# First loads, product with ones, order of a merge and last scaling of a two-layer hybrid trunk on one Trainium2 core

## Chip, core and metric

The kernel runs on one NeuronCore of one Trainium2 chip, with five engines beside the 16 DMA engines: TensorE (PE in the profile; its weight loads are PEld), VectorE (DVE), ScalarE (ACT), GpSimd (POOL) and SyncE (SP, which here only issues DMAs). The metric is the device time of one launch in microseconds; lower is better. All arithmetic is fp32, or fp32 split into two parts (below).

## What is computed

Two layers over x (1 x 512 x 1024), each a token mixer with three branches and a gated MLP, and a final RMSNorm:

```python
for l in range(2):
    h = rmsnorm(x, norm1_g[l])
    p = h @ w_in[l]                      # 1024 -> 1792 + 1536 + 1024 + 3072
    y_rw  = rwkv7_branch(p_rw, ...)      # scan over 512 steps, 8 heads of 64
    y_ret = retention_branch(p_ret, ...) # chunks of 128, 4 heads
    y_sg  = sgu_branch(p_sg, ...)        # gating with a causal 128 x 128 matrix per group, + bias
    branches = stack([y_rw, y_ret, y_sg])
    proj  = einsum('bsgc,gcd->bsgd', branches, w_branch[l])     # 512 -> 1024 each
    gates = sigmoid(gate_logits)
    x = x + sum(gates * proj, axis=2) @ w_out[l]
    x = x + conv_ffn(rmsnorm(x, norm2_g[l]), ...)               # 1024 -> 5632 -> 1024
return rmsnorm(x, final_g)
```

In `sgu_branch` the vector v is normalised over its 512 channels with `sg_ln_g` and `sg_ln_b` and then mixed by the masked matrix w; the constant `sg_ln_b` comes through the mixing as the row sums of w times `sg_ln_b`.

## The kernel before

**Layout.** Activations lie transposed, features on the 128 partitions and the 512 positions along the row; x is eight blocks of 128 x 512. A product of fp32 values is made of three fp32r matmuls: each operand is split into a high part (a cast on ACT, L127, L136 or L202) and a low part (the difference, on DVE, L128, L137 or L203), and `mm3` (L140) adds high x low, high x high and low x high in PSUM. Some small products stay fp32 (the transposes, the ones product at L848, retention's chunks).

**Weights** stream in units of 128 x 512 floats (256 KB). `load` (L112) issues a unit's DMA on SP's queue into one of three raw buffers `wr`; `part` (L120) splits it. `unit` (L89) keeps loads and splits a few units ahead of PE by a plan that a first pass over the program records. The tile framework's scheduler then sets the order of the instructions on each engine; what is wrapped in `keep_in_program_order` (`self.kept`, `po`) or in `high_priority` keeps its written place. Semaphores are placed by the framework wherever two engines touch a tile; tiles of a pool are handed out again in turn, so a new tile waits for the last user of the buffer's old one. PSUM has four accumulators `acc` and four small tiles `sm`.

**Start (`run`, L258).** DVE fills `rst` with ones, and PE runs six fp32 products on it as a warm-up (L269). `load_pc(0)` (L304) brings the layer's 250 columns of per-channel factors (norm gains, mixing factors, decay factors and so on; `pc`, 125 KB) on ACT's queue; behind it x1 and x3 go on ACT's queue, the other x blocks and the first weights on SP's. Then a step list written out by hand sets the order on ACT and DVE: `z` is a block of `norm_z` (L199: x times gain, split), `w` a weight split, `s` a square and its sum (`norm_sq`, L206). The sums go into `norm_stats` (L216), a product with ones on PE, in the middle of the first projection (`firstF`, L233). At the top of `rwkv` (L384) five small DVE products make derived factors from `pc` (`omu`, `haw`, `hka`, `oka`, `nkk`; L390 to L398). L505 later writes zeros into some columns of `rst`, which the scan uses as its reset mask.

**Mixer (L308).** While the recurrence's small products run, PE is filled with projections. Then come the spatial gating's values (`sgu_v`), its bias (`sgu_bias`, L843), the recurrence's output, and the merge, whose order is a step list at L332:

```python
for step in "S S 0 0 R U S 0 R 0 U S 0 0 R 0 0 R 2 2 Y 2 1 2 1 2 1 2 1 2 1 2 1 1 1".split():
```

`S` is a group of spatial gating, `R` a chunk of retention (`ret_chunk`, L754; small fp32 products, with normalisation through ACT, DVE and a power on GpSimd at L781), `U` two units of a projection, `Y` the transposition and split of retention's heads (`ret_out`, L802, transposes at L807). `0`, `2` and `1` are blocks of `merge` (L864) for the recurrence, the spatial gating and retention: the gate values come by a DMA on GpSimd's queue (L868), twelve matmuls go into an `acc`, DVE multiplies by the gate (L871), and `2` adds to the block's sum on GpSimd, `1` on DVE (L874). A block `1` needs `Y`.

`sgu_bias` multiplies the masked 128 x 4 x 128 gating matrix `ws` by a 128 x 128 tile of ones in one fp32 product; `ws` is masked at L325.

**End (`finish`, L945).** The last of the eight output blocks of the second MLP is computed in two halves of 256 positions, so that the first half's normalisation runs beside the second half's matmuls. For a half, `stats` sums the squares and takes the power -1/2 on GpSimd (L974), `out` spreads the result over the partitions by transposes into the PSUM tile `pb` (L980), and `scale` forms eight products x * gain * pb on DVE (L986), each sent out by a 128 KB DMA, alternately on ACT's and SP's queue (L987).

Of the kernel before, what the change touches and what calls it, by code (L numbers as in the profile page):

```python
# [17 lines left out]
S = 512  # L18
# [28 lines left out]
class Emit:  # L47
# [210 lines left out]
    def run(self):  # L258
        nc, tc, a, V = self.nc, self.tc, self.a, self.nc.vector
        self.con = self.cp.tile([128, NCC], F32, name="con")  # L260
        self.rst = self.cp.tile([128, 512], F32, name="rst")
        self.bonesR = self.cp.tile([128, 128], F32R, name="bonesR")
        self.ones = self.cp.tile([128, 128], F32, name="ones")
        V.memset(self.rst, 1.0)
        V.memset(self.ones, 1.0)
        nc.scalar.copy(self.small((128, 1), "ms"), self.rst[:, 0:1])
        wu = self.acc()
        for i in range(6):
            nc.tensor.matmul(wu[:, 0:256], self.rst[:, 0:128], self.rst[:, 256:512], start=True, stop=True)  # L269
        self.load_pc(0)  # L270
        st = self.norm_new()
        xs = [self.u(n="x") for _ in range(8)]
        self.keep = True
        with tc.high_priority():
            for j in range(8):
                tc.keep_in_program_order((nc.scalar if j in (1, 3) else nc.sync).dma_start(xs[j], a["xT"][:, j, :]))
                if self.plan and j in (0, 2, 3):
                    self.load(self.plan[self.nraw])
        for step in "z0 w z1 z2 w z3 w z4 z5 w z6 z7 w s0 s1 s2 w s3 s4 s5 s6 s7".split():
            if step == "w":  # L280
                if self.plan:
                    if self.nraw == self.npart:
                        self.load(self.plan[self.nraw])
                    self.part(self.plan[self.npart])
            elif step[0] == "z":
                self.norm_z(st, xs[int(step[1])], "n1")
            else:
                self.norm_sq(st, xs[int(step[1])])
        self.keep = False
        tc.keep_in_program_order(nc.scalar.dma_start(self.con, a["con"]))  # L290
        xd = [a["xT"][:, j, :] for j in range(8)]
        for l in range(L):
            mg = self.mixer(l, st)
            st = self.norm_new()
            x = self.wout(l, mg, xd, st)
            act = self.ffn_up(l, st)
            st = self.norm_new()
            x, xd = self.ffn_down(l, act, x, st)
            if l == L - 1:
                self.finish(l, act, x, st["acc"])  # L300
            self.rp.__exit__(None, None, None)
            self.fp = None
# [5 lines left out]
    def mixer(self, l, nst):  # L308
        self.pool = None
        with self.tc.tile_pool(name=f"rw{l}", bufs=1) as rp:  # L310
            self.rwp = rp
            self.filler = self.fillers(l)
            st = self.rwkv(l, nst)
        for _ in self.filler:
            pass
        self.rp = self.tc.tile_pool(name=f"ff{l}", bufs=NFP)
        self.fp = self.rp.__enter__()
        self.gup, self.bs, self.ws = self.f(n="gup"), self.f((128, 4, 128), n="bs"), self.f((128, 4, 128), n="ws")
        with self.tc.high_priority():
            self.nc.sync.dma_start(self.gup, self.a["gup"][l])  # L320
        self.nc.sync.dma_start(self.bs.rearrange("p g i -> p (g i)"), self.a["sgb"][l:l + 1, :].to_broadcast([128, 512]))
        self.nc.sync.dma_start(self.ws, self.a["sgw"][l])
        self.pool = "f"
        sg, out = self.sgu_v(l), self.rwkv_out(l, *st)
        self.nc.vector.tensor_tensor(self.ws, self.ws, self.c("le").unsqueeze(1).to_broadcast([128, 4, 128]), op=MUL)  # L325
        for step in (sg, sg, out, sg, None, out, sg, out, out):
            next(step) if step else self.sgu_bias()
        yrw, ysg, mg, out, m2 = self.yrw, [], [], [], 0
        self.ret_heads()
        self.pool = "r"  # L330
        rest, chunk = self.sgu_u(l, range(2, 4)), iter(range(NC))
        for step in "S S 0 0 R U S 0 R 0 U S 0 0 R 0 0 R 2 2 Y 2 1 2 1 2 1 2 1 2 1 2 1 1 1".split():  # L332
            if step == "S":
                ysg.append(self.sgu_out(len(ysg)))
            elif step == "R":
                self.ret_chunk(next(chunk))
            elif step == "U":
                next(rest), next(rest)
            elif step == "Y":
                yret = self.ret_out()  # L340
            elif step == "0":
                mg.append(self.merge(l, 0, len(mg), yrw))
            elif step == "2":
                mg[m2] = self.merge(l, 2, m2, ysg, mg[m2])
                m2 += 1
            else:
                out.append(self.split(self.merge(l, 1, len(out), yret, mg[len(out)], self.nc.vector), self.f))
        return out
# [35 lines left out]
    def rwkv(self, l, nst):  # L384
# [2 lines left out]
        q8 = lambda t: t.rearrange("p (c t) -> p c t", t=64)  # L387
        pcol = lambda n, w: self.pc[:, PC[n]:PC[n] + w]
        omu = self.small((128, 14), "omu", bufs=1)
        V.tensor_scalar(omu, pcol("mu", 14), -1.0, 1.0, op0=MUL, op1=ADD)  # L390
        haw = self.small((128, 8), "haw")
        V.tensor_scalar(haw, pcol("a0", 8), 0.5, None, op0=MUL)
        hka = self.small((128, 4), "hka")
# [449 lines left out]
    def sgu_bias(self):  # L843

        nc, V = self.nc, self.nc.vector
        bs, ws = self.bs, self.ws
        pb = self.sm((128, 4, 128))
        nc.tensor.matmul(pb, self.ones, ws, start=True, stop=True)  # L848
        for g in range(4):
            V.scalar_tensor_tensor(bs[:, g, :], pb[:, g, :], self.p("sb", g), bs[:, g, :], op0=MUL, op1=ADD)  # L850

# [93 lines left out]
    def finish(self, l, act, x, acc):  # L945

        nc, V, A, T = self.nc, self.nc.vector, self.nc.scalar, self.nc.tensor
        self.pool = "u"
        w = [self.unit("wdn", l, 7, k * 512, min(512, DFF - k * 512)) for k in range(6)]
        po = self.tc.keep_in_program_order  # L950
        pt = self.sm((128, 4))
        hs = [slice(0, 256), slice(256, 512)]
        pss = [self.acc((128, 256)) for _ in range(2)]

        def prod(h, k0, k1):
            for k in range(k0, k1):
                ks = slice(k % 4 * 128, k % 4 * 128 + 128)
                (wh, wl), (xh, xl) = w[k // 4], act[k]
                self.mm3(pss[h], (wh[:, ks], wl[:, ks]), (xh[:, hs[h]], xl[:, hs[h]]), k == 0, k == NFF - 1)

        def square(h):
            xi = x[7][:, hs[h]]
            po(V.scalar_tensor_tensor(xi, pss[h], 0.5, xi, op0=MUL, op1=ADD))
            sq = self.u((128, 256), n="sq")
            A.activation(sq, xi, AF.Square)
            return sq

        def stats(h, sq):
            for e in range(2):
                c = 2 * h + e  # L970
                po(T.matmul(pt[:, c:c + 1], sq[:, 128 * e:128 * e + 128], self.c("ones"), start=False, stop=True, skip_group_check=True))
            ms, rs = self.small((128, 2), "ms"), self.small((128, 2), "rs")
            po(V.tensor_scalar(ms, pt[:, 2 * h:2 * h + 2], 1.0 / D, 1e-6, op0=MUL, op1=ADD))
            nc.gpsimd.tensor_tensor(rs, ms, self.c("mhalf")[:, 0:2], op=POW)  # L974
            return rs

        def out(h, rs):
            pb = self.sm((128, 256))
            for e in range(2):
                po(T.transpose(pb[:, 128 * e:128 * e + 128], rs[:, e:e + 1].to_broadcast([128, 128]), self.c("ident")))  # L980
            return pb

        def scale(h, pb, js):
            for j in js:
                t = self.u((128, 256), n="o")
                po(V.scalar_tensor_tensor(t, x[j][:, hs[h]], self.p("fg", j), pb, op0=MUL, op1=MUL))  # L986
                (nc.sync if j % 2 else nc.scalar).dma_start(self.a["out"][:, j, hs[h]], t)  # L987

        self.pin = True
        prod(0, 0, 8)  # L990
        for c in range(NC):
            po(T.matmul(pt[:, c:c + 1], acc[:, 128 * c:128 * c + 128], self.c("ones"), start=c == 0, stop=False, skip_group_check=True))
        prod(0, 8, NFF)
        sq = square(0)
        prod(1, 0, 4)
        rs = stats(0, sq)
        prod(1, 4, 8)
        pb = out(0, rs)
        scale(0, pb, range(8))
        prod(1, 8, NFF)  # L1000
        rs = stats(1, square(1))
        scale(1, out(1, rs), range(8))

# [109 lines left out]
```

## Time and profile before

| what | value |
|---|---|
| median of 3 runs | 1775.89 us (1774.39 to 1777.48) |
| the profiled execution | 1773.46 us |
| its span | 1771.4 us |
| granted TensorE clock | 0.999 |
| PE busy | 1755.7 us (99%) |
| DVE, ACT, POOL busy | 1161.9 (66%), 784.6 (44%), 192.7 us (11%) |
| moved by DMA | 193.27 MB, 109 GB/s on average |

Times in the profile's rows are microseconds from the start of the span. A row of the timeline has start, duration, engine, line, operation, output and inputs, shapes and count, and in brackets the idle time before it with what ended it; a row with a count covers that many instructions, from the first one's start to the last one's end. An engine name ending in q (SPq, ACTq) is a DMA being issued. A row of groups has count, busy time, mean ns of one, and the idle time before. Ends of matmuls are modelled and overlap the next; the distance between starts tells how long PE is held.

### The profile page before, as it was taken

The numbers are of one execution on the slowest core, as the hardware profiler recorded it, in microseconds if no ns is written. First come the engines' busy times: TensorE is split into PE (matmuls) and PEld (weight loads), VectorE is DVE, ScalarE is ACT, GpSimd is POOL, SyncE is SP. The second block draws the span as 40 slices with busy tenths as digits, with TensorE's granted clock in tenths as the row PEclk, the third lists the DMA queues.
The fourth block names the chain that finished last, engine by engine and source line by source line (L and its number), as shares of the span: only waits on it lengthen the run. The fifth ranks groups of instructions, "written<-read, shape, count | busy, mean of one in ns | idle before, by whom it ended". The sixth has DMA issues, their size and how long they took to land.

```text
span 1771.4 us, 25916 instructions
## 1 busy us (share of the span) xinstructions
PE 1755.7 (99%) x9646; PEld 1442.4 (81%) x9646; DVE 1161.9 (66%) x1996; ACT 784.6 (44%) x1333; POOL 192.7 (11%) x240
## 2 busy tenths in 40 slices
PE   9999999999999999999999999999999999999998
PEld 7878887888888888888887788778888888888887
DVE  6887736468767777753358876465676687777433
ACT  5564444544344444443245544445332454443321
POOL 0132012013300000000002220220132000000000
PEclk9999999999999999999999999999999999999999
DMA  4234432324542232243322343323154422221332
GB/s 168 78 95 143 131 108 74 113 71 157 170 137 96 96 101 96 71 119 111 108 94 72 115 142 119 102 78 132 54 169 151 148 97 95 96 97 64 113 96 84
DMA packets 104109, 193.27 MB, mean 109 GB/s; under 512 B 11952, under 2 KB 16304, under 8 KB 103984
## 3 DMA queue, kind: packets, MB, share of 16 engines
q1 hardware_dynamic: 89280, 159.42, 27.9%
q10 hardware_dynamic: 10224, 17.52, 2.9%
q0 software_dynamic: 4480, 14.68, 2.5%
q8 instruction: 76, 1.25, 0.3%
q14 instruction: 49, 0.40, 0.1%
HBM read 174.80 MB, written 16.78 MB: 108 GB/s over the span
## 4 chain that ended last, share of the span: by engine, by line
PE 97%; ACT 1%; issue 1%; DVE 1%; DMA 0%; POOLq 0%; POOL 0%; DVEq 0%
PE acc L144 89%; PE sm L561 1%; PE sm L486 1%; PE sm L442 1%; PE sm L568 1%; PE sm L577 0%; PE sm L591 0%; PE sm L856 0%; PE sm L772 0%; PE sm L761 0%; PE sm L453 0%; PE sm L551 0%; PE sm L687 0%; DMA x<-xT 0%; PE sm L144 0%
## 5 line engine op out<-in xcount | busy, mean ns | idle before, releaser
L144 PE MATMUL acc<-lo,sh 128*128 128x512 f32 x1056 | 414.8, 393 | 2.0 <-DVE lo L137 1.2
L144 PE MATMUL acc<-hi,sh 128*128 128x512 f32 x1056 | 413.8, 392 | 0.0
L144 PE MATMUL acc<-hi,sl 128*128 128x512 f32 x1056 | 412.1, 391 | 0.0
L127 ACT CAST sh<-wr 128x512 fp32r<-128x512 f32 x376 | 228.2, 611 | 380.6 <-PE acc L144 284.4
L128 DVE TENSOR_TENSOR sl<-wr,sh 128x512 fp32r<-128x512 f32 x376 | 257.8, 689 | 181.4 <-PE acc L144 99.8
L144 PE MATMUL acc<-lo,wh 128*128 128x512 f32 x640 | 253.3, 396 | 2.4 <-DVE rst L505 1.5
L144 PE MATMUL acc<-hi,wh 128*128 128x512 f32 x640 | 250.8, 392 | 0.0
L144 PE MATMUL acc<-hi,wl 128*128 128x512 f32 x640 | 249.8, 392 | 0.0
L144 PEld LDWEIGHTS acc<-lo,sh 128*128 128x128 f32 x1056 | 198.5, 188 | 44.3 <-issue 2.9
L127 ACT CAST wh<-wr 128x512 fp32r<-128x512 f32 x208 | 128.5, 619 | 237.1 <-PE acc L144 220.8
L144 PEld LDWEIGHTS acc<-hi,sl 128*128 128x128 f32 x1056 | 198.5, 188 | 40.9
L144 PEld LDWEIGHTS acc<-hi,sh 128*128 128x128 f32 x1056 | 198.6, 188 | 40.1
L128 DVE TENSOR_TENSOR wl<-wr,wh 128x512 fp32r<-128x512 f32 x208 | 150.7, 725 | 120.3 <-ACT wh L127 117.2
L144 PE MATMUL acc<-ah,sh 128*128 128x512 f32 (+1 forms) x748 | 219.6, 377 | 0.0
L144 PEld LDWEIGHTS acc<-ah,sh 128*128 128x128 f32 x748 | 137.8, 188 | 25.8
L144 PEld LDWEIGHTS acc<-lo,wh 128*128 128x128 f32 x640 | 120.3, 188 | 29.6 <-ACT wh L127 1.9
L144 PEld LDWEIGHTS acc<-hi,wl 128*128 128x128 f32 x640 | 120.3, 188 | 26.8 <-issue 1.1
L144 PE MATMUL acc<-ah,sl 128*128 128x512 f32 (+1 forms) x374 | 141.0, 377 | 0.0
L144 PEld LDWEIGHTS acc<-hi,wh 128*128 128x128 f32 x640 | 120.4, 188 | 25.2 <-issue 1.1
L907 DVE TENSOR_TENSOR fu<-acc,rsF 128x512 f32<-128x512 f32 x88 | 60.8, 690 | 69.4 <-PE acc L144 69.3
L909 ACT ACTIVATE cv<-fu,pc 128x512 f32<-128x512 f32 x88 | 71.8, 816 | 44.1 <-DVE fu L907 39.3
L144 PEld LDWEIGHTS acc<-ah,sl 128*128 128x128 f32 x374 | 70.4, 188 | 12.7
(277 smaller groups left out, 2169.5 us busy)
## 6 DMA issues: line engine op xcount, KB each, us to landing
wr<-wall SPq DMA_DIRECT2D x488, 256.0 KB, 2.6
wr<-wdn SPq DMA_DIRECT2D x80, 256.0 KB, 2.6
gd<-gth ACTq DMA_DIRECT2D x48, 256.0 KB, 3.2
gth<-gd POOLq DMA_DIRECT2D x48, 256.0 KB, 3.4
tab<-rot ACTq DMA_DIRECT2D x8, 256.0 KB, 3.3
xi<-xT SPq DMA_DIRECT2D x8, 256.0 KB, 3.1
wr<-wdn SPq DMA_DIRECT2D x16, 128.0 KB, 2.1
xd<-xi POOLq DMA_DIRECT2D x8, 256.0 KB, 2.7
```

Of the source, the lines that this page charges most:

```text
L127: self.kept(self.nc.scalar.copy(hi[:, :n], raw[:, :n]))
L128: self.kept(self.nc.vector.tensor_tensor(lo[:, :n], raw[:, :n], hi[:, :n], op=SUB))
L144: i = self.nc.tensor.matmul(*x, **y)
L442: T.matmul(o, w[ks, ms], x[ks, :], start=i == 0, stop=i == 2)
L486: T.matmul(pgs[h][:, j, :], bk[hv[h], c, :, :].rearrange("p a t -> p (a t)"), ag[hv[h], h, c, :], start=True, stop=True)
L561: po(T.matmul(o[hv[h], m, :], AG[m][:, h, c, i:i + 64], w[:, m, h, :], start=m == 0, stop=i == 0, skip_group_check=True))
L568: po(T.matmul(pu[hv[h], 0, m, :], GB[:, 8 * m + c, 0:64], ub[:, m, h, :], start=m == 0, stop=True, skip_group_check=True))
L907: V.tensor_tensor(u, ps, self.rsF, op=MUL)
L909: A.activation(t, u, AF.Identity, scale=self.p("cw2", j), bias=self.p("cb", j))
```

## The change

Five edits in one. (1) At the start the eight columns of norm gains are loaded alone (into a tile `g1` that takes the place of `pc` until then), first on ACT's queue; the table load and the first copies of ACT come behind its three DMAs, the whole `pc` behind the squares; the warm-up has five products; `omu` of the first layer keeps its written place; and the step list brings x3's split ahead of the second weight split. (2) `ones` becomes an fp32r tile made by a copy, and the masked `ws` is split, so that the bias product is two fp32r matmuls. (3) In the merge's step list one `0` between the last two `R` and one before them move behind `Y`. (4) In the last half's scaling, three of the eight blocks are multiplied by their gain ahead of time on ACT (`gx`), `pb` is copied to SBUF by ACT, and GpSimd makes those three products; DVE makes five. (5) The output DMAs are divided between the queues as three (ACT) and five (SP). The instruction order of both programs on PE differs only in these places; on DVE the memset of `rst` (L505) comes to stand ahead of the first split, and four of the five small products on `pc` stand between the sums of squares. In the last half DVE's first product waits for ACT's copy of `pb`.

```diff
-        self.ones = self.cp.tile([128, 128], F32, name="ones")
+        self.ones = self.cp.tile([128, 128], F32R, name="ones")
         V.memset(self.rst, 1.0)
-        V.memset(self.ones, 1.0)
-        nc.scalar.copy(self.small((128, 1), "ms"), self.rst[:, 0:1])
         wu = self.acc()
-        for i in range(6):
+        for i in range(5):
             nc.tensor.matmul(wu[:, 0:256], self.rst[:, 0:128], self.rst[:, 256:512], start=True, stop=True)
-        self.load_pc(0)
+        self.pc = self.sp.tile([128, 64], F32, name="g1", tag="g1", bufs=1)
...
         with tc.high_priority():
+            tc.keep_in_program_order(nc.scalar.dma_start(self.pc[:, 0:8], a["pcols"][0][:, PC["n1"]:PC["n1"] + 8]))
             for j in range(8):
...
-        for step in "z0 w z1 z2 w z3 w z4 z5 w z6 z7 w s0 s1 s2 w s3 s4 s5 s6 s7".split():
+        tc.keep_in_program_order(nc.scalar.copy(self.small((128, 1), "ms"), self.rst[:, 0:1]))
+        tc.keep_in_program_order(nc.scalar.copy(self.ones, self.rst[:, 0:128]))
+        for step in "z0 w z1 z2 z3 w w z4 z5 w z6 z7 w s0 s1 s2 w s3 s4 s5 s6 s7".split():
...
         self.keep = False
+        self.load_pc(0)
         tc.keep_in_program_order(nc.scalar.dma_start(self.con, a["con"]))
...
         self.nc.vector.tensor_tensor(self.ws, self.ws, self.c("le").unsqueeze(1).to_broadcast([128, 4, 128]), op=MUL)
+        self.wsp = self.split(self.ws.rearrange("p g i -> p (g i)"), self.f)
...
-        for step in "S S 0 0 R U S 0 R 0 U S 0 0 R 0 0 R 2 2 Y 2 1 2 1 2 1 2 1 2 1 2 1 1 1".split():
+        for step in "S S 0 0 R U S 0 R 0 U S 0 R 0 R 2 2 Y 0 0 2 1 2 1 2 1 2 1 2 1 2 1 1 1".split():
...
-        V.tensor_scalar(omu, pcol("mu", 14), -1.0, 1.0, op0=MUL, op1=ADD)
+        po = self.tc.keep_in_program_order if l == 0 else lambda i: i
+        po(V.tensor_scalar(omu, pcol("mu", 14), -1.0, 1.0, op0=MUL, op1=ADD))
...
-        nc.tensor.matmul(pb, self.ones, ws, start=True, stop=True)
+        for i in (1, 0):
+            nc.tensor.matmul(pb, self.ones, self.wsp[i], start=i == 1, stop=i == 0)
...
-        def scale(h, pb, js):
-            for j in js:
+        def scale(h, pb):
+
+            if gx:
+                pbs = self.u((128, 256), n="pbs")
+                po(A.copy(pbs, pb))
+            order = [j for i in range(4) for j in ((i, i + 3) if i < 3 else (6, 7))] if gx else range(8)
+            for j in order:
                 t = self.u((128, 256), n="o")
-                po(V.scalar_tensor_tensor(t, x[j][:, hs[h]], self.p("fg", j), pb, op0=MUL, op1=MUL))
-                (nc.sync if j % 2 else nc.scalar).dma_start(self.a["out"][:, j, hs[h]], t)
+                if gx and j < 3:
+                    nc.gpsimd.tensor_tensor(t, gx[j], pbs, op=MUL)
+                else:
+                    po(V.scalar_tensor_tensor(t, x[j][:, hs[h]], self.p("fg", j), pb, op0=MUL, op1=MUL))
+                (nc.scalar if j in (1, 4, 6) else nc.sync).dma_start(self.a["out"][:, j, hs[h]], t)
...
         pb = out(0, rs)
-        scale(0, pb, range(8))
+        scale(0, pb)
+        for j in range(3):
+            t = self.u((128, 256), n="gx")
+            A.activation(t, x[j][:, hs[1]], AF.Copy, scale=self.p("fg", j))
+            gx.append(t)
         prod(1, 8, NFF)
         rs = stats(1, square(1))
-        scale(1, out(1, rs), range(8))
+        scale(1, out(1, rs))
```

More of the change, by code (lines that the diff above doesn't have):

```diff
@@ L845, in sgu_bias @@
         nc, V = self.nc, self.nc.vector
-        bs, ws = self.bs, self.ws
+        bs = self.bs
         pb = self.sm((128, 4, 128))
-        nc.tensor.matmul(pb, self.ones, ws, start=True, stop=True)
+        for i in (1, 0):
+            nc.tensor.matmul(pb, self.ones, self.wsp[i], start=i == 1, stop=i == 0)
         for g in range(4):
@@ L952, in finish @@
         hs = [slice(0, 256), slice(256, 512)]
-        pss = [self.acc((128, 256)) for _ in range(2)]
+        pss, gx = [self.acc((128, 256)) for _ in range(2)], []
         def prod(h, k0, k1):
```

## The prediction

> **What bounds the kernel now.** I read the page first: the span, the busy row, the shares of the chain that ended last.
>
> ```profile
> span 1771.4 us, 25916 instructions
> PE 1755.7 (99%) x9646; PEld 1442.4 (81%) x9646; DVE 1161.9 (66%) x1996; ACT 784.6 (44%) x1333; POOL 192.7 (11%) x240
> PE 97%; ACT 1%; issue 1%; DVE 1%; DMA 0%; POOLq 0%; POOL 0%; DVEq 0%
> ```
>
> PE carries the chain, and the change takes almost no matmul away, so its worth lies where PE waits: the start, one place of the merge in each layer, and the end, where the chain leaves PE. The profiled execution took 1773.46 us, 2.06 more than its span; the median of the runs, 1775.89, is 2.43 above it. I sum on the profile and apply the sum to the median. Under 0.2% (3.55 us) is about what a measurement of this kernel cannot tell from no change.
>
> Next the timeline of the first 12 us, and then the chain of waits in order of time:
>
> ```profile
> 0.81 1.28 ACT L266 ACT_TABLE_LOAD   x1 [0.81 <-PEq L1103]
> 1.51 0.39 ACTq L306 DMA_DIRECT2D pc<-pcols  x1
> 1.53 4.50 PE L269 MATMUL acc<-rst 128*128 128x256 f32 x12 [1.53 <-DVE rst L264]
> 5.88 0.72 ACT L202 ACTIVATE hi<-x,pc 128x512 fp32r<-128x512 f32 x1 [3.59 <-DMA pc<-pcols]
> 6.51 0.60 ACT L127 CAST wh<-wr 128x512 fp32r<-128x512 f32 x1
> 7.32 0.68 DVE L128 TENSOR_TENSOR wl<-wr,wh 128x512 fp32r<-128x512 f32 x1
> 7.34 0.07 DVE L505 MEMSET rst<- 128x8 f32 x1
> 7.53 0.47 PE L144 MATMUL acc<-lo,wh 128*128 128x512 f32 x1 [1.50 <-DVE rst L505]
> 8.39 1.41 DVE L203 SCALAR_TENSOR_TENSOR lo<-x,pc,hi 128x512 fp32r<-128x512 f32 x2 [0.39 <-ACT hi L202]
> 11.12 0.51 PE L144 MATMUL acc<-lo,wh 128*128 128x512 f32 x1 [0.26 <-DVE lo L203]
> ```
>
> ```profile
> 11.12 14.60 PE acc L144 x63
> 25.72 0.79 PE sm L220 x8
> 29.83 10.23 PE acc L144 x45
> ```
>
> ACT idles 3.59 us until all 250 columns of factors have landed; only then are x and weights split and multiplied. From 11.12, where the fourth x block (x3) is ready, PE runs on without a gap, one 512-column matmul in 10.23/45 = 0.227 us. The start is worth what 11.12 moves.
>
> **Start.** Issue and landing of x0 (SP), of x1 and x3 (ACT), and of the factors in both layers:
>
> ```profile
> L276 SPq DMA_DIRECT2D x<-xT x1: 378/378/378, 0.8 to 0.8; - x1
> DMA to landing us min/median/max: 2.9/2.9/2.9
> ```
>
> ```profile
> L276 ACTq DMA_DIRECT2D x<-xT x2: 445/449/453, 1.9 to 2.4; - x2
> DMA to landing us min/median/max: 5.7/6.3/6.8
> ```
>
> ```profile
> L306 ACTq DMA_DIRECT2D pc<-pcols x2: 334/362/391, 1.5 to 768.7; - x2
> DMA to landing us min/median/max: 2.0/3.1/4.3
> ```
>
> Eight columns go out first on ACT, from 0.81, and land 2.0 to 4.3 later, at 2.8 to 5.1; x0 lands at 3.7. x1 and x3 are issued some 0.7 earlier, and 125 KB no longer run ahead of them: x3, at 2.4 + 6.8 = 9.2 today, I place at 7.5 (the four blocks x0, w0, the factors and x1 landed about 1 us apart, so one place less and 0.7). The table load now follows three issues of 0.45: 2.15 to 3.43, then two short copies; ACT is free at about 3.9 instead of 5.88 for the first split.
>
> What is late next is DVE. Its small memset of rst (L505) now stands ahead of the first split, and it overwrites what the warm-up reads, so DVE waits for the warm-up's end: 6.03 with six products, with five between 5.28 (4.50/6 less) and 5.65 (the last ones are shorter); I take 5.6. Behind it on DVE: lo of x0, lo of w0, lo of x1, x2, x3. Four steps of 0.68 and a last of 0.75 end at 5.7 + 2.7 + 0.75 = 9.15; PE starts x3 at 9.2. ACT's side (split of x0, weights, x1, x2, x3; 0.6 to 0.72 each) ends by 8.2 with x3 landed at 7.5, so it hides; with the eight columns only at 5.1 it ends at 8.6, which costs 0.2. Gain 11.12 - 9.2 = **1.9**. Bounds: the memset at 5.28 gives 2.3; x3 landing at 8.5 (only the earlier issue helps) gives 8.5 + 0.72 + 0.75, PE at 10.0, gain 1.1.
>
> The full factors now go out behind the squares, ahead of the constants and wua on ACT's queue, at 17.4 - 1.9 = 15.5, and land at 17.5 to 19.8; five small DVE products on them wait there in front of the last four sums of squares. The sums must be through when PE reaches the statistics (25.72 now, 23.8 then):
>
> ```profile
> 17.39 0.34 ACTq L290 DMA_DIRECT2D con<-con  x1
> 22.23 0.68 DVE L210 TENSOR_TENSOR sq<-sq,sq 128x512 f32<-128x512 f32 x1
> ```
>
> Last sum ends 22.91 - 1.9 = 21.0, plus 0.1 to 2.4 of wait and about 0.6 for the small products: 21.7 to 24.0. Cost 0, at worst 0.2.
>
> **Product with ones**, and the split that it now needs:
>
> ```profile
> 371.48 1.02 PE L848 MATMUL sm<-ws,ones 128*128 128x512 f32 x2
> 372.33 0.60 PE L622 MATMUL sm<-con,y 128*128 128x128 f32 x4
> ```
>
> ```profile
> 333.93 0.69 DVE L325 TENSOR_TENSOR ws<-ws,con 128x512 f32<-128x512 f32 x1 [1.87 <-DMA ws<-sgw]
> 335.47 0.62 ACT L127 CAST wh<-wr 128x512 fp32r<-128x512 f32 x1 [2.10 <-PE acc L144]
> ```
>
> From 371.48 to 372.33 the fp32 product holds PE 0.85 us; two fp32r ones take 2 x 0.227 = 0.455. Saved 0.40 a layer, **0.8** for two. The split (0.62 on ACT, 0.69 on DVE) falls at 334.6 into ACT's 2.10 of idle time, 37 us before its use; if that gap were gone, a weight cast would come 0.6 later, and casts run two units of 2.7 us ahead of PE. Cost 0.
>
> **Merge.** Both layers show the same stall, behind the transposes of ret_out:
>
> ```profile
> 441.70 0.38 PE L807 MATMUL sm<-con,sgg 128*128 128x128 f32 x2
> 442.69 0.50 PE L144 MATMUL acc<-lo,sh 128*128 128x512 f32 x1 [0.60 <-DVE lo L137]
> ...
> 1318.00 0.38 PE L807 MATMUL sm<-con,sgg 128*128 128x128 f32 x2
> 1318.98 0.50 PE L144 MATMUL acc<-lo,sh 128*128 128x512 f32 x1 [0.60 <-DVE lo L137]
> ```
>
> The first block on the transposed heads needs their split (ACT then DVE, 0.6 and 0.69); the last two transposes take some 0.17, and PE resumes 0.99 after they began, so 0.82 is lost. The two moved blocks now stand among the transposes instead of among the last retention chunks. In the changed order PE has four matmuls (0.9 us) between the last transposes and that first block, and, more to the point, twelve (2.7 us) between the first head's last transpose and it; a split takes 1.3, and the block uses the heads one after the other, 0.7 us apart: each is ready about 0.9 us ahead of use. The stall goes. Fp32 and fp32r runs alternate 11 times instead of 13; the first matmul after fp32 costs about 0.1 more, so another 0.1 to 0.2. But retention chunks come closer together, and an add on GpSimd collides with DVE splits. I take 0.9 a layer, **1.8**; bounds 0.6 and 1.1 a layer.
>
> **End.** The second half's scaling, its transfers, and the nearest rows for what is added:
>
> ```profile
> 1765.26 3.22 DVE L986 SCALAR_TENSOR_TENSOR o<-xi,pc,sm 128x256 f32<-128x256 f32 x8 [1.30 <-PE sm L980]
> ```
>
> ```profile
> 1766.60:1769.80 3.20, 0.00 (x0) 0.00 (x0) 1.88 (x5) 0.00 (x0) 0.00 (x0) 0.50 0.97 327
> ```
>
> ```profile
> L774 ACT COPY ry<-sm 128x256 f32<-128x256 f32 x16 | 5.8, 364 | 5.3 <-PE sm L772 5.2
> L588 POOL TENSOR_TENSOR fS<-cs,F 64x256 f32<-64x256 f32 x24 | 17.8, 742 | 35.2 <-DVE cs L584 27.9 <-DVE cs L582 6.5
> ```
>
> DVE delivers a piece each 0.39 us, and the window row shows the 16 DMA engines busy for 0.97 of the 3.2 us in which these pieces go out: the transfers are full. GpSimd's three pieces (0.74 each by L588) finish the arithmetic sooner, but at most 0.03 x 3.2 = 0.1 of transfer time can be won. Against it, in the changed order DVE's first piece waits for ACT's copy of pb, because both read the same PSUM tile: 0.36 and a semaphore, 0.4 later for the first transfer. The Trainium skill, PSUM — Partial Sum Buffer, section "PSUM bank collisions raise a hardware error", says that two engines must not read one bank at once, reads against reads included, so they have to be ordered. No run here shows such a collision; by that rule the wait is inherent in this sharing, and with free sharing the same sum would be 0.4 better. Net **-0.3** (a loss); bounds -0.6 (a GpSimd piece comes last) and +0.1. The gx products on ACT lie under PE's second half, which runs to 1762.
>
> Sum: 1.9 + 0.8 + 1.8 - 0.3 = 4.2 us less; 1773.46 becomes 1769.3, the median 1775.89 becomes **1771.7**. With all ends good 2.3 + 0.8 + 2.2 + 0.1 = 5.4 (1770.5), with all bad 1.1 - 0.2 + 0.8 + 1.2 - 0.6 = 2.3 (1773.6).
>
> **Rivals.** (a) *The loads come no sooner*: x3 and the weights are held by the 16 DMA engines, not by the factors' 125 KB, and the start gains 0.7 instead of 1.9. For: x1 to x3 already land one after the other. Against: ACT's 3.59 idle for pc alone. Sum 3.0, 1772.9. Chance 0.14.
>
> (b) *The shorter warm-up leaves the clock low.* Against it: the warm-up's row quickens within its six products:
>
> ```profile
> L269 PE MATMUL acc<-rst x12: 379/635/794, 1.5 to 5.7; 128*128 128x256 f32 x12
> ```
>
> Durations fall from 0.79 to 0.38, so speed came late in the 4.5 us, and one product less leaves little behind it. If x0 to x2's nine matmuls ran at twice 0.227, they would take 4.1 from 6.5, PE would reach x3 at 10.6, and 1.4 is lost: sum 2.8, 1773.1. Chance 0.08. The Trainium skill, TensorE: Matmul & The Clock Gate, section "What's actually happening", speaks against this edit: full clock needs a busy window of about 3.4 us whose phase is free. By that rule it is chance whether five products suffice; the quickening in the row agrees with it.
>
> (c) *Slower: the moved blocks wait for their accumulators.* Their gate loads stand on GpSimd's queue behind the last chunk's powers and adds, and their DVE products behind four head splits and a weight split; PE needs the accumulator back four blocks later.
>
> ```profile
> gth<-gd POOLq DMA_DIRECT2D x48, 256.0 KB, 3.4
> ```
>
> I count the load in 4 us ahead of use and the DVE product some 0.3 us ahead of PE. With a wait W in each layer in place of the 1.8, the change is 2.4 - 2W: slower from W = 1.2, that is if these DVE products come 1.5 later than I count. At W = 3.3 it costs 4.2: 1780.1. Against: L871 today never holds PE here. Chance 0.05.
>
> (d) *All good ends*: 5.2, 1770.7. Chance 0.11. The forecast keeps 0.62.
>
> **How the numbers follow.** Four fifths of the forecast's 0.62 lie beyond 3.55, and all of (d): 0.50 + 0.11 = 0.61 faster. Within 0.2%: 0.12 + 0.14 + 0.08 = 0.34. Slower: 0.05. The range 1769.7 to 1774.6 takes the bounds 1770.5 and 1773.6 and about 0.9 for a median of three whose runs spread 3.1; it leaves out (c) and the tails.
>
> **What would show it.** In the profile after: ACT's first x split near 4 and not 5.88; the memset of rst before DVE's first lo, ending near 5.7; the unbroken PE chain from 9.2; the ones product 0.46 apart; no idle before the first block behind the heads' transposes, near 440 and 1315; the first DVE piece of the end 0.4 after the transposes, DMA again full. Wrong if that chain starts at 10 or later, if PE waits for a DVE gate product behind the moved blocks, or if the clock is still low at 6.5.

## Result and the profile after

| | before | after |
|---|---|---|
| median of 8 runs | 1774.39 us (1773.37 to 1777.48) | 1769.39 us (1768.82 to 1770.18) |
| profiled execution (span) | 1773.46 us (1771.4) | 1769.48 us (1767.7) |
| ratio after to before, 95% interval | | 0.9969 [0.9959, 0.998] |

The change saves 5.0 us by the medians and 4.0 by the profiled executions. The forecast was 1771.7, with a range down to 1769.7; the measured median lies 0.3 below that range. The median of before, on which the forecast put its sum, was 1775.89 from three runs and is 1774.39 from eight; so of the 2.3 by which the forecast missed, 1.5 lie in the base and 0.8 in the saving (5.0 against 4.2).

**A ledger.** The same instruction is looked up in both traces, and its two starts are subtracted.

| start of | before | after | difference | this stretch |
|---|---|---|---|---|
| ones product, layer 0 | 371.48 | 370.29 | -1.19 | start: -1.19 |
| the product behind it (L622, L626) | 372.33 | 370.75 | -1.58 | ones: -0.39 |
| statistics behind the merge, layer 0 | 533.42 | 530.16 | -3.26 | merge: -1.68 |
| ones product, layer 1 | 1247.78 | 1244.55 | -3.23 | +0.03 |
| the product behind it | 1248.63 | 1245.00 | -3.63 | ones: -0.40 |
| statistics behind the merge, layer 1 | 1409.76 | 1404.15 | -5.61 | merge: -1.98 |
| last transposes (L980, L985) | 1764.79 | 1759.18 | -5.61 | 0 |
| end of the span | 1771.4 | 1767.7 | -3.7 | end: +1.9 |

So the start gave 1.2, the ones 0.8, the merge 3.7, and the end took 1.9 back. (What lies outside the span is 2.06 in the one execution and 1.78 in the other; in the kernels below it is 1.6 to 2.1 and about the same in all runs of a kernel. The first edit, the third and the end, each alone, have 0.2 to 0.4 less of it than the kernel before; why is open.)

**Start.** The chain of waits of after, in order of time, and then rows of its timeline:

```profile
1.25 5.69 DMA x<-xT
...
8.53 16.00 PE acc L144 x69
24.52 0.79 PE sm L220 x8
```

```profile
1.52 4.63 PE L267 MATMUL acc<-rst 128*128 128x256 f32 x10 [1.52 <-DVE rst L264]
...
4.36 0.72 ACT L202 ACTIVATE hi<-x,g 128x512 fp32r<-128x512 f32 x1 [0.46 <-DMA g<-pcols]
...
6.29 0.07 DVE L509 MEMSET rst<- 128x8 f32 x1 [4.83 <-PE acc L267]
6.39 0.75 DVE L203 SCALAR_TENSOR_TENSOR lo<-x,g,hi 128x512 fp32r<-128x512 f32 x1
6.96 1.95 ACT L202 ACTIVATE hi<-x,g 128x512 fp32r<-128x512 f32 x3 [0.86 <-DMA x<-xT]
...
8.53 0.50 PE L144 MATMUL acc<-lo,wh 128*128 128x512 f32 x1 [0.23 <-DVE lo L203]
```

ACT's first split stands at 4.36 (5.88 before), and the factors hold it only 0.46. But DVE's small memset waits for the warm-up until 6.29, as the five products ran at the low clock to their end, and x1 lands only at 6.94 (1.25 + 5.69). The statistics come 1.20 earlier (25.72 to 24.52).

**Ones and merge.** PE's timeline of after, at the ones product of layer 0 and behind the heads' transposes in both layers:

```profile
370.29 0.39 PE L853 MATMUL sm<-lo,ones 128*128 128x512 f32 x1
370.51 0.39 PE L853 MATMUL sm<-hi,ones 128*128 128x512 f32 x1
370.75 0.60 PE L626 MATMUL sm<-con,y 128*128 128x128 f32 x4
```

```profile
439.21 0.38 PE L811 MATMUL sm<-con,sgg 128*128 128x128 f32 x2
439.35 0.48 PE L144 MATMUL acc<-hi,sl 128*128 128x512 f32 x1
```

```profile
1313.47 0.38 PE L811 MATMUL sm<-con,sgg 128*128 128x128 f32 x2
1313.61 0.48 PE L144 MATMUL acc<-hi,sl 128*128 128x512 f32 x1
```

The ones take 0.46 in place of 0.85. Behind the two transposes PE goes on after 0.14 where it needed 0.99. That is half of the merge's gain. The other half shows where the merge's gate product on DVE (L871, L876 after) is asked who waited for it; first before, then after:

```profile
who waited for it (us, times):
  POOL gth L874: 58.1, 14
  PE acc L144: 0.8, 4
```

```profile
who waited for it (us, times):
  POOL gth L879: 41.3, 10
  PEld acc L144: 0.3, 1
```

Before, PE waited four times for a gate product to give its accumulator back; after, no matmul does, and one weight load does (at 443.19 in layer 0, where two matmuls come 0.2 late together). Two of the four places lie in each merge, where its steps alternate between 2 and 1. The rows of before in layer 0:

```profile
473.27 0.47 PE L144 MATMUL acc<-lo,sh 128*128 128x512 f32 x1 [0.21 <-DVE gth L871]
...
479.16 0.47 PE L144 MATMUL acc<-lo,sh 128*128 128x512 f32 x1 [0.16 <-DVE gth L871]
```

Behind the matmuls of 472.67 and 478.61 these start 0.37 and 0.32 later than the usual 0.23. With the 0.85 behind the transposes that makes 1.5 of a layer's gain; the rest, 0.1 and 0.4, is not assigned.

**End.** The timeline of after from the copy of `pb` on, and of each kernel the closing rows of GpSimd's and SyncE's queues (count: shortest/median/longest in ns, first start to last start; the longest is the first to start); before those of before stands its last GpSimd instruction:

```profile
1759.71 0.37 ACT L992 COPY pbs<-sm 128x256 f32<-128x256 f32 x1 [2.28 <-PE sm L985]
1760.11 2.05 DVE L999 SCALAR_TENSOR_TENSOR o<-xi,pc,sm 128x256 f32<-128x256 f32 x5 [1.76 <-ACT pbs L992]
1760.16 2.09 POOL L997 TENSOR_TENSOR o<-gx,pbs 128x256 f32<-128x256 f32 x3 [1.03 <-ACT pbs L992]
```

```profile
L1123 POOLq DRAIN  x3: 40/93/6789, 1760.1 to 1767.4; - x3
L1123 SPq DRAIN  x3: 7/7/7, 1765.4 to 1767.2; - x3
```

```profile
1764.04 0.69 POOL L974 TENSOR_TENSOR rs<-ms,con 128x2 f32<-128x2 f32 x1 [7.72 <-DVE ms L973]
```

```profile
L1106 POOLq DRAIN  x3: 40/93/5396, 1764.0 to 1771.2; - x3
L1106 SPq DRAIN  x3: 7/7/7, 1770.6 to 1770.9; - x3
```

Each program closes with a drain on every engine (the rows named DRAIN) and a barrier (rows of semaphores). GpSimd's drain starts early and ends 4.7 us behind GpSimd's last instruction: 1764.0 + 5.4 = 1769.4 against 1764.73 before, 1760.1 + 6.8 = 1766.9 against 1762.25 after. SyncE, which waits for all transfers to land, is through at 1770.6 before and at 1765.4 after. So before the transfers ended last, by 1.2; after, the drain does, by 1.5. GpSimd used to finish with the power of the statistics; now its three products come later. With the first piece 0.46 later (0.93 behind the transposes instead of 0.47), that is the 1.9.

### The profile page after: what moved, and what is told of

Its sections match the earlier page's. It is cut to its first block, busy times and chain, and to the rows that moved or that the text cites. A ratio compares the mean times of both kernels' runs of the same rounds, so it can differ in the third digit from the quotient of the medians.

```text
span 1767.7 us, 25922 instructions
## 1 busy us (share of the span) xinstructions
PE 1753.0 (99%) x9644; PEld 1441.2 (82%) x9644; DVE 1159.4 (66%) x1994; ACT 788.6 (45%) x1340; POOL 196.5 (11%) x243
## 3 DMA queue, kind: packets, MB, share of 16 engines
q8 instruction: 76, 1.25, 0.3%
## 4 chain that ended last, share of the span: by engine, by line
PE 98%; ACT 1%; DMA 0%; DVE 0%; issue 0%; POOL 0%; POOLq 0%; ACTq 0%; DVEq 0%
PE acc L144 89%; PE sm L565 1%; PE sm L490 1%; PE sm L446 1%; PE sm L572 1%; PE sm L581 0%; PE sm L595 0%; PE sm L861 0%; PE sm L776 0%; PE sm L765 0%; PE sm L457 0%; PE sm L555 0%; PE sm L691 0%; DMA x<-xT 0%; PE sm L144 0%; PE sm L773 0%
```

## The experiments

| kernel | median, us | before on the same chip | ratio, 95% interval |
|---|---|---|---|
| p_start, first edit alone | 1772.23 | 1775.03 | 0.9985 [0.9976, 0.9994] |
| p_ones, second alone | 1775.46 | 1775.03 | 1.0002 [0.9993, 1.0011] |
| p_merge, third alone | 1771.31 | 1775.03 | 0.9983 [0.9974, 0.9992] |
| p_end, end alone | 1776.79 | 1775.03 | 1.0011 [1.0002, 1.002] |
| a_oldend, after with the old end | 1768.67 | 1774.84 | 0.9961 [0.9949, 0.9974] |
| a_pool1, one product on GpSimd | 1767.82 | 1774.84 | 0.9961 [0.9949, 0.9974] |
| a_wt6, old end, own warm-up tile | 1767.25 | 1774.84 | 0.9955 [0.9943, 0.9968] |
| a_wt6w, also later weights | 1767.41 | 1775.57 | 0.9949 [0.9937, 0.9962] |
| b_wu8, before, longer warm-up | 1777.60 | 1774.84 | 1.0015 [1.0006, 1.0025] |
| b_wu8r, same, loads kept early | 1774.63 | 1775.57 | 0.999 [0.9982, 0.9999] |
| b_dveadd, before, adds on DVE | 1777.00 | 1775.57 | 1.0007 [0.9998, 1.0017] |
| b_latepool, before, one late copy | 1782.64 (1 run) | 1775.57 | |

**Each edit alone.** On the kernel before: first the start,

```diff
-        for i in range(6):
+        for i in range(5):
...
-        self.load_pc(0)
+        self.pc = self.sp.tile([128, 64], F32, name="g1", tag="g1", bufs=1)
...
-        for step in "z0 w z1 z2 w z3 w z4 ...
+        for step in "z0 w z1 z2 z3 w w z4 ...
...
         self.keep = False
+        self.load_pc(0)
```

> The kernel before with the first edit alone (first loads, five warm-up products, x3's split ahead of the second weight's). Ledger (the two traces laid side by side, matmul by matmul): -1.2 us, since the 46th matmul and all behind it start 1.2 earlier. The forecast's own term: -1.9 us. If the loads came no sooner (rival a): -0.7 us.

then the ones,

```diff
+        self.wsp = self.split(self.ws.rearrange("p g i -> p (g i)"), self.f)
...
-        nc.tensor.matmul(pb, self.ones, ws, start=True, stop=True)
+        for i in (1, 0):
+            nc.tensor.matmul(pb, self.ones, self.wsp[i], start=i == 1, stop=i == 0)
```

> The kernel before with the second edit alone (ones as fp32r, the masked gating matrix split, two products). Both the ledger and the forecast: -0.8 us, 0.4 a layer. If the added split delays a weight cast that PE then waits for: 0 or slower.

the merge,

```diff
-        ... "S S 0 0 R U S 0 R 0 U S 0 0 R 0 0 R 2 2 Y 2 1 2 1 ...
+        ... "S S 0 0 R U S 0 R 0 U S 0 R 0 R 2 2 Y 0 0 2 1 2 1 ...
```

> The kernel before with the third edit alone (two blocks of the merge moved behind Y). Ledger: -3.5 us, 1.7 to 1.9 a layer, because with the stall behind the transposes (0.8) two stalls at the start of the output projection (0.37 and 0.32 a layer) go as well. The forecast's term: -1.8 us, if those two stalls went for another reason than the moved blocks.

and the end, `finish` as a whole from the changed kernel:

```diff
+                if gx and j < 3:
+                    nc.gpsimd.tensor_tensor(t, gx[j], pbs, op=MUL)
```

> The kernel before with the last scaling shared with GpSimd alone. Drain theory: +1.9 us: 0.46 because the first piece waits for ACT's copy, and 1.4 because GpSimd's closing drain ends 4.7 us behind its last product and the end of the program waits for it. The forecast's term: +0.3 us. With free sharing: -0.1 us.

Measured: -2.8, +0.4, -3.7 and +1.8 us by the medians. The merge and the end come out near the ledger's -3.5 and +1.9, but the times alone don't settle it: p_merge's interval, -4.6 to -1.4 us, holds the forecast's -1.8 too, and p_end's, +0.4 to +3.6, leaves out +0.3 only barely. The kernels' own traces do, read like the ledger against before's. p_start is 1.14 ahead at the first ones product. From the ones product to the statistics behind the merge p_ones is 0.40 and 0.47 shorter in the two layers, p_merge 1.91 and 1.94. From the last transposes to the end of the span p_end takes 8.51, as after does, and before 6.66. In p_merge no matmul and no weight load waits for a gate product any more, so that gain hangs on the moved blocks and on no other edit. (The expectation puts the two waits at the start of the output projection; they lie in the merge itself.) The closing rows of p_end:

```profile
L1118 POOLq DRAIN  x3: 40/93/6789, 1766.8 to 1774.1; - x3
L1118 SPq DRAIN  x3: 7/7/7, 1772.1 to 1773.8; - x3
```

The drain is through at 1773.6, 1.4 behind SyncE; whether it is the cause the next runs test. By its time p_ones is unclear, with an interval from -1.2 to +2.0. The start alone brought more than either account said (its interval, -4.3 to -1.1, holds both); this led to the runs on the clock.

**The end: is it the drain?** Three kernels. The first has the old `finish` in the changed kernel; the second lowers the three products on GpSimd to one, and the pieces go in plain order:

```diff
-                if gx and j < 3:
+                if gx and j < 1:
```

> The changed kernel with the end of the kernel before (all eight products on DVE, transfers alternately). Drain theory: 1.9 us less than the changed kernel (1769.4 becomes 1767.5), the closing drain of GpSimd through before the last transfer has landed. The forecast's term: 0.3 less. If sharing with GpSimd pays: 0.1 more.

> The changed kernel with one product on GpSimd and seven on DVE in place of three and five; ACT's copy of pb and the division of the transfers stay. Drain theory: GpSimd's last product ends 1.4 us earlier, its drain then about when the last transfer lands: 1.2 to 1.4 us less than the changed kernel. If the loss lies in the copy, the queues or the transfers: no change, or up to 0.5 more, since DVE has two more pieces of 0.39 us.

The third is the kernel before with one small instruction more:

```diff
-        scale(1, out(1, rs), range(8))
+        last = scale(1, out(1, rs), range(8))
+        nc.gpsimd.tensor_copy(self.small((128, 2), "lp"), last[:, 0:2])
```

> The kernel before with one tiny copy on GpSimd (128x2) behind the last of DVE's eight pieces; nothing waits for its result. Drain theory: GpSimd's closing drain ends 4.7 us behind the end of that copy (about 1768.8), 2.8 us later than the end of SyncE's waits, so the span is 2.6 to 3 us longer than before. If the drain does not follow the last instruction: span as before, or 0.1 more.

The same closing rows, of a_oldend, of a_pool1 and (with its late copy) of b_latepool:

```profile
L1111 POOLq DRAIN  x3: 40/93/5396, 1758.0 to 1765.3; - x3
...
L1111 SPq DRAIN  x3: 7/7/7, 1764.7 to 1765.0; - x3
```

```profile
L1122 POOLq DRAIN  x3: 40/93/5426, 1759.7 to 1765.6; - x3
L1122 SPq DRAIN  x3: 7/7/7, 1765.0 to 1765.4; - x3
```

```profile
1774.97 0.18 POOL L1004 COPY lp<-o 128x2 f32<-128x2 f32 x1 [3.81 <-DVE o L986]
```

```profile
L1108 POOLq DRAIN  x3: 40/102/4871, 1774.9 to 1780.3; - x3
L1108 SPq DRAIN  x3: 7/7/7, 1777.1 to 1780.1; - x3
```

In a_oldend the drain is through 1.3 us ahead of SyncE; in a_pool1 the two end together (1765.1 and 1765.0); in b_latepool the drain ends at 1779.8, 4.7 behind a copy of 0.18 us that nothing uses, and 2.7 behind SyncE. That run's whole time, 1782.64, is not read: it was some 6 us late before its end, a window at half clock and late factors among the causes, and most of that is not explained. The stretch from the last transposes to the end of the span leaves out what came ahead of it: it takes 6.66 in before, 9.39 in b_latepool (2.7 more, as expected), 8.51 in after, 7.14 in a_pool1 and 6.69 in a_oldend. By the profiled executions a_oldend has a span of 1765.5 and a_pool1 of 1765.9, against 1767.7. The medians say the same where the clock stayed up (granted 0.998 or more): the two such runs of a_oldend took 1767.20 and 1767.41, the four of a_pool1 1767.63 to 1767.83, all eight of the changed kernel 1768.82 to 1770.18. The medians in the table differ less, as three of a_oldend's five runs had a lower clock (see the clock below). The drain theory stands: the sharing is no loss by the copy or the queues, apart from the 0.5, but by what comes behind GpSimd's last product.

**The accumulators' waits.** Trace rows suggested that GpSimd's adds lengthen DVE's splits and so the gate products behind them.

```diff
-        (add or nc.gpsimd).tensor_tensor(sum, sum, t, op=ADD)
+        nc.vector.tensor_tensor(sum, sum, t, op=ADD)
```

> The kernel before with all of the merge's adds on DVE instead of eight of sixteen a layer on GpSimd. Collision theory (a split on DVE, two operands in SBUF, takes 1.2 to 1.5 us instead of 0.69 while GpSimd adds): no split in the merge over 0.8 us, and the second stall at the start of the output projection, 0.32, gone; DVE's own work grows by 0.69 for each add. If the order on DVE alone makes the stall: it stays or grows, and the time is the same or up to 2 us longer.

The groups of DVE in the later merge of layer 0, of the kernel before and of b_dveadd (mean ns of one in the fourth place):

```profile
L128 DVE TENSOR_TENSOR sl<-wr,sh 128x512 fp32r<-128x512 f32 x7 | 6.8, 974 | 3.2 <-ACT sh L127 3.2
```

```profile
L128 DVE TENSOR_TENSOR sl<-wr,sh 128x512 fp32r<-128x512 f32 x7 | 4.8, 689 | 3.0 <-ACT sh L127 3.0
```

The first half is right: in the kernel before, the three of the seven splits that start during an add on GpSimd take 1.16, 1.48 and 1.44 (the mean of all seven is 0.97), the others and all of b_dveadd's 0.69; the gate product, with one operand in PSUM, keeps 0.68 in both. The Trainium skill (GPSIMD Engine Reference, section "1. Specifications") names this contention for DVE instructions with two SBUF inputs; the rows agree. The second half fell: PE's waits in b_dveadd are still there, 0.48 and 0.48 in layer 0, with no long split ahead of them, and the kernel is 0.07% longer (its interval reaches to the same). The edit also lengthened the stall behind the transposes, from 0.88 between two matmuls to 1.64 and 1.80, so its time says nothing of the adds alone. By its rows DVE's order makes the waits: the gate product stands behind a sum, its split's 0.69 of waiting for ACT, and a weight split; with the blocks moved that order is another one. This is argued from the rows: why the scheduler's order fits better there was not taken apart.

**The start and the clock.** Why did p_start gain 2.8 where the ledger had 1.2? Its runs also scatter less. The mean granted clock is listed for every run. Of the 69 runs of before beside the experiments, 32 had 0.998 or more, with a median of 1774.38, and 37 had less, with 1775.73. Of the 29 runs with the new start (after, p_start, a_oldend, a_pool1) only 4 had less. What a lower clock looks like is seen in p_merge's profile (old start), by windows, beside before's profile. The columns are PE, PEld, DVE, ACT, POOL busy, then PEclk:

```profile
6.60:10.01 3.41, 2.09 (x7) 0.97 (x6) 2.36 (x6) 2.18 (x4) 0.00 (x0) 1.00 1.04 393
10.01:13.42 3.41, 3.41 (x10) 2.63 (x9) 3.18 (x5) 2.23 (x5) 0.00 (x0) 0.50 0.85 301
95.30:98.70 3.40, 3.40 (x18) 2.17 (x17) 2.18 (x3) 3.36 (x7) 3.27 (x4) 1.00 0.12 29
98.76:102.17 3.41, 3.41 (x10) 2.64 (x10) 3.41 (x6) 0.29 (x2) 1.08 (x1) 0.50 0.32 111
```

```profile
10.01:13.42 3.41, 3.15 (x14) 2.27 (x14) 2.98 (x5) 2.19 (x5) 0.00 (x0) 1.00 0.91 324
...
98.76:102.17 3.41, 3.41 (x17) 2.80 (x16) 3.41 (x8) 1.45 (x3) 0.00 (x0) 1.00 0.25 77
```

For 3.41 us PE runs at half clock and does 10 matmuls instead of 14 or 17, behind a stretch in which it paused, at the start (2.09 of 3.41 busy) and, in this run, behind small products of the recurrence. By the starts of the same matmuls such a window puts PE 0.8 us (p_ones, at the start) to 1.6 us (p_merge, at 98.76) behind before's trace. The Trainium skill (TensorE: Matmul & The Clock Gate, section "What's actually happening") describes a free-running window of 3413 ns; the length agrees. Busy time alone doesn't tell whether a pause costs a window: before's profile had 1.92 of 3.42 busy ahead of a window at full clock, p_merge's 2.09 ahead of one at half clock. That it hangs on where in the window the pause falls is a guess. The mean clock, too, tells of such windows only roughly: p_ones's profile has one (8.55 to 11.96) and a mean of 0.998.

If PE's pause at the start is to blame, a longer warm-up in the kernel before should close it:

```diff
+        wt = self.u((128, 256), n="wt")
+        V.memset(wt, 1.0)
         V.memset(self.rst, 1.0)
...
-        for i in range(6):
-            nc.tensor.matmul(wu[:, 0:256], self.rst[:, 0:128], self.rst[:, 256:512], start=True, stop=True)
+        for i in range(8):
+            nc.tensor.matmul(wu[:, 0:256], wt[:, 0:128], wt, start=True, stop=True)
```

> The kernel before with eight warm-up products on a tile of their own, so that PE pauses less ahead of the first block. Clock theory (PE's pauses between 5.9 and 9.2 can cost one 3.41 us window at half clock, by the phase of the window): the fastest runs as before (1773.4 to 1774), the slow half rarer, mean granted clock 0.998 or more in nearly all runs, median 0.5 to 1 us less. If the pause has nothing to do with it: median and spread as before.

This first try missed its aim: it came out 2.8 us slower.

```profile
1.78 0.38 ACTq L308 DMA_DIRECT2D pc<-pcols  x1
...
7.34 0.72 ACT L202 ACTIVATE hi<-x,pc 128x512 fp32r<-128x512 f32 x1 [5.05 <-DMA pc<-pcols]
```

The second memset delayed the issue of the factors from 1.51 to 1.78, behind x2's on the other queue (1.72), and in this execution they were there at 7.34. So its time tells of the loads and not of the clock. (Seven of its 11 runs had a clock under 0.998, and its profile has half clock from 11.14: with the factors late, PE still paused from 6.5 to 9.0, and the longer warm-up did not help.) With the two memsets exchanged the issue stays at 1.51:

> The kernel before with eight warm-up products on a tile of their own, the fill of rst ahead of it, so that the loads leave ACT's queue when they do in the kernel before; PE is at work until the first block of x is ready. Clock theory (PE's pauses between 5.9 and 9.2 cost, by the phase of the 3.41 us window, one window at half clock, 1.2 to 1.6 us): lowest time as before (1773.4), granted clock 0.998 or more in nearly all runs where it was lower in 14 of 33, median 0.5 to 1 us less. If the pauses don't matter: clock under 0.998 in about 2 runs of 5, median as before.

Now 10 of 11 runs have 0.998 or more, where 7 of the 21 runs of before beside them did; the median is 0.9 less, the lowest time (1773.43) that of before. The clock theory holds so far. (The interval, 0.9982 to 0.9999, only just leaves out no change; the count of clocks says more.)

The factors' landing is the second thing that varies. In the seven profiles in which all 250 columns were issued at 1.51, ACT's first split started at 5.07, 5.29, 5.51, 5.52, 5.88, 6.38 and 7.36; in six with the eight columns alone, at 4.30 to 4.53. The profile of before, 1773.46, was among its fastest executions (69 runs: lowest 1773.29, median 1775.13), that of after in the middle of its own. So the medians can differ by more than the ledger. Of p_start's 2.8 its trace shows 0.9 (a span of 1770.5 against 1771.4: the 1.1 of the start, less 0.2 at the end, where DVE's first piece comes later); 0.3 to 0.4 lies outside the span; and 0.5 is the clock, since the 19 of 33 runs of before beside it with 0.998 or more have a median of 1774.53 instead of 1775.03. For the remaining 1.0 the factors' landing is the candidate, but those runs left no trace, so it is not shown.

**A version that beats both.** Old end, and the warm-up on a tile of its own with six products, so that the small memset of `rst` waits for nothing; then also the second and third weight's loads later:

```diff
-                if self.plan and j in (0, 2, 3):
+                if self.plan and j in (0, 4, 5):
```

> The changed kernel with the old end, and with six warm-up products on a tile of their own, so that the small memset of rst waits for nothing. If x1's landing (6.94) ends last behind the memset: lo of x0 at about 5.1 and not 6.39, PE's unbroken run from 8.4 instead of 8.5, 0.1 to 0.2 us less than with the old end alone. If the wait for the warm-up is what the start still loses: 0.7 to 1.2 less.

> The changed kernel with the old end, six warm-up products on a tile of their own, and the second and third weight issued behind x4 and x5 instead of x2 and x3. If the 16 DMA engines set when x1 to x3 land (0.98 to 1.01 busy there): x1 to x3 land 0.5 to 1 us sooner and PE's unbroken run starts 0.3 to 0.6 sooner than in the kernel with six warm-up products alone (1767.3). If the second weight then comes last: the same or up to 1 us longer.

In a_wt6 the low part of x0 starts at 5.15 and not 6.39, x1's first matmul at 7.50, and PE's unbroken run, a block further on, 0.6 earlier than in the changed kernel and 0.5 earlier than in a_oldend, where x3 landed 0.6 later (8.30 and 7.74); neither expectation fits this. But the span, 1765.7, is no better than a_oldend's 1765.5: 0.3 and 0.2 of the lead are gone behind the two merges and another 0.2 at the end, for reasons left open. All five of its runs have a clock of 0.998 or more, 1766.80 to 1767.57. Later weights change nothing that shows (1767.41, one run of five with a low clock): x1, x2 and x3 landed at 5.79, 6.97 and 7.28 instead of 5.68, 7.07 and 7.74, and PE's run began 0.1 sooner, where 0.3 to 0.6 was expected. Against the changed kernel a_wt6 is 2.1 us less by the medians, nearly all of it from the old end.

## Why the prediction was right and wrong

The direction was right; the number missed by 2.3, 0.3 beyond the range. Of the four terms one, the ones product, had the right size.

- **The base.** The sum of 4.2 was applied to a median of three runs, 1775.89. From eight it is 1774.39. With that the forecast would have been 1770.2 and its range would have held the result. The prediction noted that median and profile stood 2.43 apart, 2.06 of it outside the span in that execution, and the spread of 3.1, but not why runs of one kernel spread so: the factors' landing and the half-clock windows, both of which the first edit lessens. A shift of the median that no single trace shows was not a case of its own.
- **Start, forecast 1.9, 1.2 by the ledger, 2.8 by the medians.** The term for the trace fell between its bound of 1.1 and the value taken. What failed is two dates of DVE's row, which ended at 9.8 and not 9.15. One is the memset's gate: "with five between 5.28 (4.50/6 less) and 5.65"; the memset stood at 6.29, because the five products stayed at the low clock to their end (4.63 us; six took 4.50). The other is the landing of the x blocks: x3, placed at 7.5, landed at 7.91, and x1, of which the sum said nothing, only at 6.94. (The step to 7.5 took four loads of before to be about 1 us apart; they landed at 3.70, 4.79, 5.79 and 7.61, with x2 between the last two.) Either date alone is enough: in after, p_start, a_oldend and a_pool1 the memset stood at 6.29, 6.14, 5.59 and 6.26 and x3 landed at 7.91, 8.41, 8.30 and 7.71, yet the low part of x3 ended at 9.80, 9.94, 9.83 and 9.69. In a_oldend the memset came when the forecast had it, and x3's landing took the gain. Rival (b) had the right cause with the wrong price: the full clock was granted at 6.7 instead of 4.9, so it was still low at 6.5, one of the forecast's own signs of being wrong, but x0's matmuls ran at full clock from 7.28, and the 1.4 was not lost.
- **Ones, 0.40 a layer.** As forecast.
- **Merge, forecast 1.8, measured 3.7.** The stall behind the transposes went as told (0.99 to 0.14). Left out was a second gain of the same size: "L871 today never holds PE here" was wrong; it held PE four times, for 0.8 in all by the profile's own answer and 1.4 by the distances between starts, and the merge gains 1.7 and 2.0 a layer. The prediction looked for accumulators' waits that the change might add (rival c) and not for those that stood there.
- **End, forecast 0.3 lost, measured 1.9.** The 0.4 for ACT's copy was right (0.46). The step that failed is that the sum ended with the last transfer. GpSimd's drain, 4.7 us behind its last instruction, had 1.2 us of cover before; GpSimd's last instruction now ends 3.1 behind the start of the transposes and not 0.06 ahead of it, which took that cover. The rows of the drain stood in the profile of before.

The errors (1.9 too little for the merge, 0.7 too much for the start, 1.6 too little for the end's loss) nearly cancel: 3.7 of the span against 4.2. The total close to the forecast is luck and no proof of its steps. (One slip in the forecast's own sums: rival (d), all good ends, has 5.2 where its sum of the good ends is 5.4.)

## What to carry to other kernels

Follow the chain past the last transfer to the end of the program: an engine's closing work counts, and GpSimd's last instruction had to end 4.7 us before SyncE was through here. When a step list is moved, ask of each resource who waits for it now, not only who might wait afterwards. When runs of one kernel spread by more than a term of the sum, find what they differ in first, and take the base from many runs.

## What was not expected of the hardware

- GpSimd's closing drain ended 4.66 to 4.67 us behind its last instruction in the traces of all fourteen kernels, whether that was a product of 128x256, a power of 128x2 or a copy of 0.18 us.
- Pauses of PE that are far shorter than 3.41 us (1.3 in p_merge, 1.9 in p_ones, in all) can be followed by a window of 3.41 us at half clock, and so can a stretch of small products in which PE shows no pause at all (95.30 to 98.70 above). The Trainium skill (TensorE: Matmul & The Clock Gate, section "Why this matters for your kernels") asks for no gaps over about 3 us; in these traces shorter ones stand ahead of half clock too.
- The factors' load, issued 1.51 us into the program beside the same other loads, had landed anywhere between 5.0 and 7.3 us.
